# A decoder block's 512-column matmuls issued as two of 256

## The chip, the core and the metric

The kernel runs on one core of a Trainium2 chip. A time is the device time of one execution in microseconds. A core has five engines with a queue of instructions each: TensorE (PE, and PEld for its weight loads), VectorE (DVE), ScalarE (ACT), GpSimd (POOL) and SyncE (SP), which issues nearly all transfers.

## The reference

One decoder block on 512 tokens of 1024 channels, in float32. Two attention branches work on the same normalised and modulated input; their projections are gated and merged, then follow an output projection, an MLP with squared ReLU and a final norm.

```python
ada = (silu(c) @ w_ada + b_ada)          # sh1, sc1, g1, sh2, sc2, g2
h = modulate(rms_norm(x, ln1_w), sh1, sc1)
mq, mk, mv, rq, rk, rv, rg, ga, gr = split(h @ w_in)
y_a = moba_attention(rope(mq), rope(mk), mv) @ w_moba_o      # 8 heads of 64
r_out = head_group_norm(retention(rope(rq), rope(rk), rv), ret_gn_w)
y_r = (silu(rg) * r_out) @ w_ret_o                           # 8 heads, V of 128
x = x + g1 * ((sigmoid(ga) * y_a + sigmoid(gr) * y_r) @ w_out)
h2 = modulate(rms_norm(x, ln2_w), sh2, sc2)
x = x + g2 * (square(relu(h2 @ w_ff1)) @ w_ff2)
return rms_norm(x, final_norm_w)
```

## The kernel before

**Products.** Every large product is made from a hi and a lo part of both operands, float32 numbers rounded for TensorE and what that leaves out. mm3 (line 211) issues the three terms hi x hi, hi x lo and lo x hi, one matmul each, into the same accumulator, a tile of 128 partitions x 512 float32, which is one bank of PSUM. The stationary operand is always 128 x 128, the moving one mostly 512 columns. The matmul's flag `start` opens an accumulation and `stop` closes it. No product names its weight load: each matmul brings its own.

**Weights.** load_w (line 175) brings 128 x 1024 numbers by SP's queue into `raw`, ScalarE makes the hi part (line 179) and GpSimd the lo part (line 181), in four buffers each.

**Stages.** In the start (to about 78 us) adaLN's shift and scale are summed on VectorE, h is made tile by tile, and the first projections (V of MoBA, one pair of Q and K) run as h comes in (lines 334 to 370). Then comes the MoBA attention (lines 868 to 889, to about 275 us): for each of 8 heads and 4 key tiles, moba_turn transposes probabilities and splits them into th and tl, moba_scores makes the next head's softmax, and moba_values multiplies th and tl with V. Between them `fill(n)` issues n steps of the projections that wait in a queue, 6 products of 512 columns a step (line 422), and `do_later(n)` issues n pieces of the rotary embedding and of the stacking of Q and K (lines 459 to 510). The retention (lines 903 to 937, to about 475 us) goes the same way. Its V (ret_values, line 600) is made by products of 256 columns, two token tiles side by side in a bank. After it come the merge with the first half of the output projection (lines 950 to 975), the second half with the second norm (1075 to 1095), the MLP's first product, channel by channel (1097 to 1132; its first four tiles are issued in two halves of 256 tokens, lines 1097 to 1102, by ff1_part), and its second, token by token (1149 to 1202), into eight banks at once: 28 k-tiles for all tokens, then the last 4 for one token tile after the other with the final norm. The last token tile's second half is taken in two parts of 256 columns (line 1201).

**What sets the order.** The order of each engine's instructions is fixed when the program is built. Within `manual_schedule` the named engines keep the order of the program's text: TensorE from the start to the end of the retention and again from the output projection's second half to ff1's halves; VectorE, ScalarE and GpSimd in the start, VectorE and ScalarE in the second of these too. Elsewhere a planner picks, from the instructions that its own model has ready, the one that stands first in the program's text. `tc.high_priority(offset=20)` (line 574) moves what moba_turn's split issues forward by 20 places in that count, over all engines. `tc.issue_after` queues work behind a given instruction.

Of the kernel before, what the change touches and what calls it, by code (L numbers as in the profile page):

```python
# [22 lines left out]
# columns of w_in  # L23
# [4 lines left out]
def block_kernel(  # L28
# [101 lines left out]
    def busy(n):  # L130
        """Keeps the tensor engine's clock up while the first operands come in."""
        for _ in range(n):
            PE.matmul(warm, ones, wide, start=True, stop=True)
# [56 lines left out]
    def load_256(w, k0, c0):  # L190
        """Rows of 4 k-tiles, 256 columns."""
        hi, lo = load_w([(lambda t: v3(t, 256), rows(w, k0, 4, c0, 256))])
        return v3(hi, 256), v3(lo, 256)

    def load_pair(w, k0, ca, cb, lo_engine=None):
        """Rows of 4 k-tiles, two groups of 128 columns."""
        hi, lo = load_w(
            [
                (lambda t: v3(t, 256)[:, :, 0:P], rows(w, k0, 4, ca, P)),
                (lambda t: v3(t, 256)[:, :, P:256], rows(w, k0, 4, cb, P)),  # L200
            ],
            lo_engine=lo_engine,
        )
        return v3(hi, 256), v3(lo, 256)

    def load_512(w, k0, c0):
        """Rows of 2 k-tiles, 512 columns."""
        hi, lo = load_w([(lambda t: v3(t, 512), rows(w, k0, 2, c0, 512))])
        return v3(hi, 512), v3(lo, 512)

    def mm3(o, lh, ll, rh, rl, first, last):
        PE.matmul(o, lh, rh, start=first, stop=False)  # L212
        PE.matmul(o, lh, rl, start=False, stop=False)  # L213
        PE.matmul(o, ll, rh, start=False, stop=last)  # L214
# [8 lines left out]
    def token_rstd(work, ss, t, tag):  # L223
        """(mean of squares + eps) ** -0.5 from the sum of squares."""
        r = work.tile([P, 2], F32, name="rstd", tag=tag, bufs=4)
        POOL.tensor_scalar(r[:, 0:1], ss, 1.0 / D, EPS, op0=ALU.mult, op1=ALU.add)
        POOL.tensor_tensor(r[:, 1:2], r[:, 0:1], mhalf, op=ALU.pow)
        return r[:, 1:2]

# [1 line left out]
    def ada_cols(hi, lo, n0, dst):  # L231
        """Column sums of hi + lo over the partitions, as columns: 128 of them into dst[:, 0:2]."""
        PE.matmul(dst, hi[:, n0 : n0 + P], ones[:, 0:2], start=True, stop=False)
        PE.matmul(dst, lo[:, n0 : n0 + P], ones[:, 0:2], start=False, stop=True)
# [20 lines left out]
    def ada_start(j):  # L255
        """adaLN's shift and scale, summed over the k-tiles partition by partition, in two halves."""
        a = [ST.tile([P, 256], F32, name="adaacc", tag="adaacc", bufs=4) for _ in range(2)]
        for k in range(2):
            ACT.activation(a[k], ada[j][:, k, :], AF.Copy, scale=cact[:, k : k + 1])
        return a  # L260
# [9 lines left out]
    def ada_columns(a):  # L270
        """The sums over the partitions, as columns."""
        cp = ps("O")
        for i in range(2):
            PE.matmul(cp[:, 2 * i : 2 * i + 2], a[0][:, i * P : (i + 1) * P], ones32[:, 0:2], start=True, stop=True)
        return cp
# [58 lines left out]
    for j in range(NK):  # L334
        _, hi, lo = wf[j]
        more = j + 1 < NK
        if j + 2 < NK:
            load_step(j + 2)

        def product(i, a, b, first, last):  # L340
            """hi or lo of h by hi or lo of the weights, for V's four tiles of tokens, Q and K."""
            w = (hi, lo)[b]
            hx = (hh, hl)[a][j]
            if i < 4:
                PE.matmul(acc_mv[i], hx[:, i * P : (i + 1) * P], w[:, 0:512], start=first, stop=last)
            else:
                c0 = 512 if i == 4 else 640
                PE.matmul((acc_q0, acc_k0)[i - 4], w[:, c0 : c0 + P], hx, start=first, stop=last)

        if more:  # L350
            ada_sum(j + 1, a, range(2, 8))
            tp = transposed(j + 1)
        for i in range(6):
            product(i, 0, 0, j == 0, False)
        for i in range(6):
            product(i, 0, 1, False, False)
            if not more:
                product(i, 1, 0, False, True)
            elif i == 2:
                cp = ada_columns(a)  # L360
                mod = modulation(j + 1, cp)
        if more:
            w_split(j + 1)
            if j + 2 < NK:
                a = ada_start(j + 2)
            else:
                first_pair = [load_pair(w_in, k0, MQ + P, MK + P, eng) for k0, eng in ((0, POOL), (4, DVE))]
            h_tile(j + 1, tp, mod)
            for i in range(6):
                product(i, 1, 0, False, False)  # L370
# [17 lines left out]
    def proj_chunks(accs, ws, nk, bh, bl):  # L388
        """Two n-tiles, channel-major, from pieces of 4 k-tiles x 256 columns: 12 products a step."""
# [16 lines left out]
    # Projections are emitted in chunks between the steps of the attention, so that the tensor  # L406
    # engine has products to go on with while a step's scores pass through the other engines. A
    # projection is a generator: first its loads, then a chunk at a time.
# [8 lines left out]
    def fill(n):  # L417
        """n steps of the projections in the queue, 6 products of 512 columns each."""
# [7 lines left out]
    def project(load, nk, bh, bl, end):  # L426
        """Two n-tiles, channel-major, from pieces of 4 k-tiles x 256 columns, one after the other."""
# [24 lines left out]
    # Work that is not urgent, emitted a little at a time after a step's own instructions.  # L452
# [6 lines left out]
    def rope(i, part, a, stack):  # L459
        """Rotary embedding of a PSUM tile, then the stacking of its result."""  # L460
# [73 lines left out]
    def moba_scores(h, t):  # L534
        """Softmax of 128 queries of a head."""
# [13 lines left out]
        if t >= 2:  # L549
            # The past block counts where its gate, q . mean(k), is finite.  # L550
# [18 lines left out]
    def moba_turn(h, kt):  # L569
        """The probabilities of 128 keys, keys on the partitions, split."""  # L570
# [27 lines left out]
    vs = {}  # L598

    def ret_values(p):  # L600
        """V of 2 heads, token-major, less its mean over each head's channels: that centres the
        retention's output, which is linear in V, for the group norm."""
# [26 lines left out]
    # A window that picks output partitions n and n + 16, the sum of such two rows to copy to all, and  # L629
    # -1 where a row is to hold a lo part.  # L630
# [70 lines left out]
    def ret_variance(h, sh, sl):  # L701
        """The sum of squares over a head's channels, into rows 32 * (h % 4) and 16 further on."""
# [12 lines left out]
    def ret_rstd(g):  # L715
        """(variance + eps) ** -0.5 of 4 heads, hi in a head's first row and lo in its second."""
# [9 lines left out]
    def ret_norm(h):  # L726
        """A head's rows, added up, to all partitions; z, split."""
# [8 lines left out]
    # adaLN rows and columns that come later: g1, sh2, sc2 (and g2), 256 columns at a time. Each  # L736
    # step of the generator adds two k-tiles of one piece, loaded two steps before; a piece's sums
    # over the partitions follow a step after its last k-tile.
# [59 lines left out]
    def advance(steps, after=None):  # L798
        """One step, its arithmetic queued behind the instruction `after`."""
        try:  # L800
            steps.send(after)
        except StopIteration:
            pass
# [7 lines left out]
    def moba_out(i2):  # L811
        """sigmoid(ga) * (the MoBA branch's projection), two n-tiles: two projections."""
# [189 lines left out]
    def load_late(k):  # L1002
        """A k-tile of the second half of w_out, in the place of h."""
# [30 lines left out]
    def turn2(t):  # L1034
        """A normalized token tile to channels on the partitions, shifted and scaled."""
# [27 lines left out]
    # A token tile's transposition follows a good part of the products of the next ones.  # L1063
# [96 lines left out]
    def final(t, parts):  # L1160
        """The last terms of a token tile, residual and final norm, a part of the columns at a time."""
# [54 lines left out]
def _constants():  # L1216
    """Tables that depend on the shapes alone: rotary cos and signed sin (channel-major, two heads
    of 64), the retention's decay with its scale, the causal cap of a diagonal block, the identity."""
# [44 lines left out]
```

## Time and profile before

| | us |
|---|---|
| runs | 946.2, 950.24, 953.29 |
| median | 950.24 |
| span of the profiled execution | 943.5 |
| TensorE matmul, busy | 892.6 |
| TensorE weight load, busy | 716.0 |
| VectorE, busy | 549.0 |
| GpSimd, busy | 425.8 |
| ScalarE, busy | 365.7 |

The span goes from the first to the last instruction of one execution; the profile lists no other time of that execution. Matmuls are pipelined: a matmul's row gives its start and a modelled end that reaches over the next one's start, so the pace of a sequence is read from its starts, and a busy share of 100% says only that no gap was longer than that overlap. The weight load of the next matmul lies beside the one that runs. PEclk is the clock granted to TensorE, as a share of 2.4 GHz; its other level, 0.5, is 1.2 GHz.

### The profile page before, as it was taken

What the parts mean: (1) busy time and instruction counts of PE and PEld (TensorE: products, weight loads), DVE (VectorE), ACT (ScalarE), POOL (GpSimd) and SP (SyncE); (2) the same over time, 40 slices, a digit from 0 to 9 for tenths busy, and PEclk for the clock granted to TensorE, in tenths of its full rate; (3) what the DMA queues carried; (4) which work ended last, traced back from release to release, by engine and by line L of the source; (5) the groups of instructions that cost most, each with busy time, mean ns of one, the idle gap of its engine ahead of it and who ended that gap; (6) DMA issues with size and microseconds to landing.
All of it is one profiled execution on the core that took longest, in us unless ns stands there. A gap on an engine that the chain in (4) does not pass through costs nothing.

```text
span 943.5 us, 11349 instructions
## 1 busy us (share of the span) xinstructions
PE 892.6 (95%) x4138; PEld 716.0 (76%) x4138; DVE 549.0 (58%) x964; ACT 365.7 (39%) x617; POOL 425.8 (45%) x231
## 2 busy tenths in 40 slices
PE   6888999988999999989999898999999999999996
PEld 4766777667877878767888687888888888888885
DVE  5877887889796787996448867701423012211135
ACT  5444555554543434544531433422222321211124
POOL 4453242233353333433453633866566554444443
PEclk9998999899999999999999998999999999999999
DMA  9944121121135424341254362533432223222212
GB/s 288 296 147 124 46 90 45 67 89 46 45 118 164 135 87 145 109 130 52 90 176 151 126 240 81 170 107 93 148 117 89 90 90 106 95 89 90 93 42 89
DMA packets 104423, 108.38 MB, mean 115 GB/s; under 512 B 4832, under 2 KB 93232, under 8 KB 104368
## 3 DMA queue, kind: packets, MB, share of 16 engines
q1 hardware_dynamic: 104224, 107.41, 35.9%
q8 instruction: 32, 0.52, 0.2%
q10 hardware_dynamic: 144, 0.26, 0.1%
q14 instruction: 23, 0.19, 0.1%
HBM read 105.55 MB, written 2.10 MB: 114 GB/s over the span
## 4 chain that ended last, share of the span: by engine, by line
PE 61%; DVE 24%; DMA 5%; issue 4%; ACT 3%; POOL 1%; SPq 1%; ACTq 0%; POOLq 0%; DVEq 0%
PE ps_acc L212 16%; PE ps_acc L213 15%; PE ps_acc L214 15%; DVE adaacc L264 2%; DMA ada_raw<-in_w_ada_dram 2%; DVE qs L489 2%; PE ps_S L214 2%; PE ps_S L213 2%; PE ps_S L212 2%; DVE qs L490 2%; DVE kl L506 1%; DVE tl L221 1%; DVE pr L560 1%; DMA raw<-in_w_ff_dram 1%; ACT sw L466 1%
## 5 line engine op out<-in xcount | busy, mean ns | idle before, releaser
L181 POOL TENSOR_TENSOR wlo<-raw,whi 128x1024 fp32r<-128x1024 f32 x125 | 307.3, 2463 | 338.5 <-ACT whi L179 310.5
L179 ACT ACTIVATE whi<-raw 128x1024 fp32r<-128x1024 f32 x126 | 132.5, 1057 | 206.9 <-PE ps_O L214 108.7
L212 PE MATMUL ps_acc<-hh,whi 128*128 128x512 f32 x304 | 127.4, 419 | 0.4 <-DVE mod L763 0.4
L214 PE MATMUL ps_acc<-hh,wlo 128*128 128x512 f32 x304 | 121.3, 399 | 0.0
L213 PE MATMUL ps_acc<-hl,whi 128*128 128x512 f32 x304 | 120.8, 397 | 0.0
L212 PE MATMUL ps_acc<-h2h,whi 128*128 128x512 f32 (+1 forms) x288 | 107.3, 373 | 0.0
L213 PE MATMUL ps_acc<-h2l,whi 128*128 128x512 f32 (+1 forms) x288 | 107.2, 372 | 0.0
L214 PE MATMUL ps_acc<-h2h,wlo 128*128 128x512 f32 (+1 forms) x288 | 107.0, 371 | 0.0
L220 DVE CAST fh<-act 128x512 fp32r<-128x512 f32 x32 | 14.9, 472 | 138.4 <-PE ps_O L213 138.4
L212 PEld LDWEIGHTS ps_acc<-hh,whi 128*128 128x128 f32 x304 | 58.2, 191 | 17.6 <-issue 5.1
L214 PEld LDWEIGHTS ps_acc<-hh,wlo 128*128 128x128 f32 x304 | 58.2, 192 | 13.6
L213 PEld LDWEIGHTS ps_acc<-hl,whi 128*128 128x128 f32 x304 | 58.4, 192 | 10.3
L213 PEld LDWEIGHTS ps_acc<-h2l,whi 128*128 128x128 f32 x288 | 54.9, 191 | 10.1 <-DVE h2l L221 0.2
L214 PEld LDWEIGHTS ps_acc<-h2h,wlo 128*128 128x128 f32 x288 | 54.9, 191 | 10.1
L212 PEld LDWEIGHTS ps_acc<-h2h,whi 128*128 128x128 f32 x288 | 55.0, 191 | 9.9
L755 DVE TENSOR_TENSOR g<-g,ps_acc 128x256 f32<-128x256 f32 x8 | 3.3, 417 | 88.9 <-PE ps_acc L754 88.9
L213 PE MATMUL ps_acc<-wlo,fh 128*128 128x512 f32 (+1 forms) x136 | 52.7, 387 | 0.0
L212 PE MATMUL ps_acc<-whi,fh 128*128 128x512 f32 (+1 forms) x136 | 52.7, 387 | 0.0
L214 PE MATMUL ps_acc<-whi,fl 128*128 128x512 f32 (+1 forms) x136 | 52.6, 387 | 0.0
L779 DVE SCALAR_TENSOR_TENSOR ada_acc<-ada_raw,cact,ada_acc 128x256 f32<-128x256 f32 x48 | 36.5, 760 | 21.4 <-DMA ada_raw<-in_w_ada_dram 20.4
L1115 POOL TENSOR_TENSOR act<-relu 128x512 f32<-128x512 f32 x32 | 34.9, 1094 | 29.9 <-ACT relu L1114 29.9
L782 DVE SCALAR_TENSOR_TENSOR ada_acc<-ada_raw,cact,ada_acc 128x256 f32<-128x256 f32 x64 | 44.7, 699 | 1.7
(283 smaller groups left out, 1924.5 us busy)
## 6 DMA issues: line engine op xcount, KB each, us to landing
raw<-in_w_ff_dram SPq DMA_DIRECT2D x64, 512.0 KB, 3.3
raw<-in_w_in_dram SPq DMA_DIRECT2D x32, 512.0 KB, 3.5
ada_raw<-in_w_ada_dram SPq DMA_DIRECT2D x64, 256.0 KB, 2.7
raw<-in_w_in_dram SPq DMA_DIRECT2D x36, 256.0 KB, 3.4
wada<-in_w_ada_dram SPq DMA_DIRECT2D x32, 256.0 KB, 5.2
x<-in_x_dram SPq DMA_DIRECT2D x8, 512.0 KB, 4.6
raw<-in_w_ret_o_dram SPq DMA_DIRECT2D x8, 512.0 KB, 3.4
dec<-in_k_decay_dram SPq DMA_DIRECT2D x8, 256.0 KB, 3.7
```

What stands on the lines that cost most here:

```text
L179: ACT.activation(hi, raw, AF.Copy)
L181: eng.tensor_sub(lo, raw, hi.bitcast(F32))
L212: PE.matmul(o, lh, rh, start=first, stop=False)
L213: PE.matmul(o, lh, rl, start=False, stop=False)
L214: PE.matmul(o, ll, rh, start=False, stop=last)
L220: eh.tensor_copy(hi, src)
L264: DVE.scalar_tensor_tensor(a[k % 2], ada[j][:, k, :], cact[:, k : k + 1], a[k % 2], op0=ALU.mult, op1=ALU.add)
L489: DVE.tensor_copy(q[own, s, :], t[own, :])
L490: DVE.tensor_sub(q[other, s, :], t[own, :], q[own, s, :].bitcast(F32))
L779: eng.scalar_tensor_tensor(acc, raw[:, 0, :], cact[:, 2 * k2 : 2 * k2 + 1], acc, op0=ALU.mult, op1=ALU.add)
L782: eng.scalar_tensor_tensor(acc, raw[:, 1, :], cact[:, 2 * k2 + 1 : 2 * k2 + 2], acc, op0=ALU.mult, op1=ALU.add)
L1115: POOL.tensor_mul(act[n], r, r)
```

## The change

mm3 and the first projections go through a new helper, product_256, which issues a product in parts of at most 256 columns, one after the other, with the same stationary operand. Only the first part of the first term carries `start`, and only the last part of the last term `stop`. Products of 256 columns or fewer come out as they were. The attention's scores, values and transposes, adaLN's sums and the start's filler matmuls (`busy`) don't go through the helper. The diff's other lines take out comments and docstrings and are left out here.

```diff
+    def product_256(o, l, r, first, last):
+
+
+        n = r.shape[-1]
+        for c0 in range(0, n, 256):
+            c1 = min(c0 + 256, n)
+            PE.matmul(o[:, c0:c1], l, r[:, c0:c1], start=first and c0 == 0, stop=last and c1 == n)
+
     def mm3(o, lh, ll, rh, rl, first, last):
-        PE.matmul(o, lh, rh, start=first, stop=False)
-        PE.matmul(o, lh, rl, start=False, stop=False)
-        PE.matmul(o, ll, rh, start=False, stop=last)
+        product_256(o, lh, rh, first, False)
+        product_256(o, lh, rl, False, False)
+        product_256(o, ll, rh, False, last)
...
             if i < 4:
-                PE.matmul(acc_mv[i], hx[:, i * P : (i + 1) * P], w[:, 0:512], start=first, stop=last)
+                product_256(acc_mv[i], hx[:, i * P : (i + 1) * P], w[:, 0:512], first, last)
             else:
                 c0 = 512 if i == 4 else 640
-                PE.matmul((acc_q0, acc_k0)[i - 4], w[:, c0 : c0 + P], hx, start=first, stop=last)
+                product_256((acc_q0, acc_k0)[i - 4], w[:, c0 : c0 + P], hx, first, last)
```

## Rows read from the trace of the kernel before

**Rows 1.** the page's head and its first part, busy time by engine

```profile
span 943.5 us, 11349 instructions
PE 892.6 (95%) x4138; PEld 716.0 (76%) x4138; DVE 549.0 (58%) x964; ACT 365.7 (39%) x617; POOL 425.8 (45%) x231
```

**Rows 2.** stretches: busy us (x instructions) of PE PEld DVE ACT POOL, PEclk, DMA share, GB/s

```profile
78.00:275.00 197.00, 178.57 (x842) 140.09 (x840) 168.41 (x384) 101.34 (x217) 66.77 (x33) 0.95 0.22 69
...
475.00:530.00 55.00, 55.00 (x240) 44.22 (x239) 37.64 (x52) 14.68 (x21) 25.51 (x13) 1.00 0.50 167
530.00:575.00 45.00, 38.33 (x174) 30.52 (x173) 34.51 (x48) 16.60 (x30) 20.96 (x12) 0.96 0.50 171
575.00:600.00 25.00, 25.00 (x204) 24.82 (x205) 19.84 (x31) 9.57 (x19) 11.39 (x8) 0.94 0.35 107
600.00:755.00 155.00, 155.00 (x670) 125.13 (x669) 38.91 (x41) 45.75 (x59) 99.58 (x57) 1.00 0.37 115
755.00:900.00 145.00, 145.00 (x623) 116.22 (x622) 28.05 (x50) 28.88 (x28) 63.83 (x28) 1.00 0.27 95
900.00:944.00 44.00, 36.00 (x167) 29.36 (x165) 18.00 (x32) 14.15 (x32) 19.37 (x13) 0.96 0.17 60
```

**Rows 3.** the chain of waits by line, of 78-275, 275-330, 330-475, 475-530, 575-944 us

```profile
by line: PE ps_acc L212 8.9%; PE ps_acc L213 7.4%; PE ps_acc L214 7.1%; DVE qs L490 6.5%; DVE pr L560 6.1%; DVE kl L506 5.9%; DVE qs L489 5.7%; DVE tl L221 4.4%; ACT sw L466 3.7%; issue 3.3%; DVE stat L556 3.3%; DVE roped L478 3.0%; PE ps_S
...
by line: PE ps_acc L212 25.0%; issue 22.0%; PE ps_acc L214 21.9%; PE ps_acc L213 21.8%; POOL wlo L181 6.2%; PE ps_S L680 4.9%; PE ps_O L689 2.3%; PE ps_O L690 2.3%; PE ps_S L679 2.3%; PE ps_O L688 2.1%; PE ps_acc L234 0.8%; PE ps_PT L709 0.
...
by line: PE ps_acc L212 16.9%; PE ps_acc L214 15.0%; PE ps_acc L213 14.9%; issue 11.0%; DVE qs L489 3.0%; PE ps_S L680 2.6%; DVE tl L221 2.4%; DVE ada_acc L782 2.3%; DVE kh L502 2.0%; DVE sl L221 2.0%; DMA ada_raw<-in_w_ada_dram 1.8%; DVE a
...
by line: DMA ada_raw<-in_w_ada_dram 31.6%; DVE ada_acc L779 10.0%; DVE ada_acc L782 10.0%; DMA raw<-in_w_out_dram 10.0%; DVE ml L959 6.5%; issue 5.5%; DVE m L957 5.2%; POOL wlo L181 4.7%; POOL wol L221 4.7%; PE ps_acc L212 2.5%; PE ps_acc L
...
by line: PE ps_acc L213 24.4%; PE ps_acc L214 24.4%; PE ps_acc L212 24.3%; PE ps_S L214 4.1%; PE ps_S L213 4.0%; PE ps_S L212 4.0%; PE ps_PT L214 2.0%; PE ps_PT L213 2.0%; PE ps_PT L212 2.0%; PE ps_O L214 1.8%; PE ps_O L212 1.8%; PE ps_O L2
```

**Rows 4.** PE in time: start us, us; first and last of 43 starts, ff1 and ff2

```profile
645.02 0.40 PE L214 MATMUL ps_acc<-h2h,wlo 128*128 128x512 f32 x1
...
654.82 0.39 PE L214 MATMUL ps_acc<-h2h,wlo 128*128 128x512 f32 x1
...
800.15 0.39 PE L212 MATMUL ps_acc<-whi,fh 128*128 128x512 f32 x1
...
809.96 0.39 PE L212 MATMUL ps_acc<-whi,fh 128*128 128x512 f32 x1
```

**Rows 5.** PE in time, ff1's halved tiles: first and last of 82 starts

```profile
589.77 0.28 PE L214 MATMUL ps_acc<-h2h,wlo 128*128 128x256 f32 x1
...
598.95 0.28 PE L214 MATMUL ps_acc<-h2h,wlo 128*128 128x256 f32 x1
```

**Rows 6.** PE in time, retention's V (33 starts), last token tile (23 starts)

```profile
366.76 0.28 PE L212 MATMUL ps_acc<-whi,hh 128*128 128x256 f32 x1
...
370.53 0.28 PE L214 MATMUL ps_acc<-whi,hl 128*128 128x256 f32 x1
...
933.13 0.28 PE L213 MATMUL ps_acc<-wlo,fh 128*128 128x256 f32 x1
...
935.72 0.28 PE L214 MATMUL ps_acc<-whi,fl 128*128 128x256 f32 x1
```

**Rows 7.** PE in time, output projection: first and last of 10 starts

```profile
546.71 0.39 PE L213 MATMUL ps_acc<-wol,mh 128*128 128x512 f32 x1
...
548.75 0.39 PE L213 MATMUL ps_acc<-wol,mh 128*128 128x512 f32 x1
```

**Rows 8.** DMA queues: packets, MB, share of 16 engines; TensorE's instruction queue

```profile
q8 instruction: 32, 0.52, 0.2%
```

**Rows 9.** 78-275 us: VectorE's groups (busy us, mean ns), and one of PE's waits

```profile
L221 DVE TENSOR_TENSOR tl<-ps_PT,th 128x512 fp32r<-128x512 f32 (+3 forms) x32 | 15.4, 481 | 0.5 <-ACT th L218 0.3
...
L490 DVE TENSOR_TENSOR qs<-roped,qs 64x512 fp32r<-64x512 f32 x12 | 14.2, 1180 | 0.4
...
PE ps_O L582 <- DVE tl L221: 4.7, 6, 1.3
```

## The prediction

> **What bounds the kernel now.** I read the page's head first: TensorE is busy 95% of a span of 943.5 us, VectorE 58%, and 4138 matmuls stand beside as many weight loads, so every matmul carries a load of its own [rows 1]. The share is an average over unlike stages, so next I read the stretches and the chain of waits of each. In the MoBA stage (78 to 275 us) TensorE is busy 178.6 of 197 us, but VectorE 168.4, and only 23.4% of the chain lies in the products of lines 212 to 214; the rest is VectorE and ScalarE work between them [rows 2, 3]. From 275 to 475 us the products hold 68.7% of 55 us and 46.8% of 145 us. In the merge (475 to 530) the chain runs over adaLN's loads (31.6%) and VectorE, though TensorE never rests, and from 530 to 575 TensorE is busy 38.3 of 45 us. From 575 to the end TensorE is busy without a break but for the last 8 us, and lines 212 to 214 with their accumulators make up nearly the whole chain [rows 2, 3]. There a nanosecond per product is a nanosecond of the kernel; elsewhere it is mostly one of waiting.
>
> **The change, part by part.** mm3 and the first projections now issue each product of 512 columns as two of 256. Products that are 256 wide already stay: the retention's V (384), the first four tiles of ff1 (192) and the last 512 columns of the last token tile (24). Split are 144 of the first projections, 912 + 96 channel-major ones, 192 of the merge, 96 + 96 of the output projection, 672 of ff1 (28 tiles x 8 x 3) and 672 + 84 of ff2: 2964. In the stage that TensorE bounds it is 672 + 756 = 1428.
>
> What a product costs is read from starts, since the ends are modelled. In ff2 42 steps take 9.81 us, in ff1 42 take 9.80: 233.3 ns each, with the clock at 1.00, its 2.4 GHz level [rows 2, 4]. Products of 256 columns run in the same program: in ff1's halved tiles 81 steps take 9.18 us, 113.3 ns each [rows 5]. Two are 226.7 ns, 6.7 less than one of 512. But 256 has a second pace: 32 steps of the retention's V take 3.77 us, 117.8 ns, without a wait among them, and 22 at the very end take 2.59 us, 117.7 ns [rows 6]. Two of those are 235.6 ns, 2.3 more than one of 512. And 512 has a faster pace as well: in the output projection 9 steps take 2.04 us, 226.7 ns [rows 7], just twice 113.3. So it isn't the width alone; a stretch settles in a pace and keeps it.
>
> For ff1 I take 113.3, since its halves have the same operands and the same accumulators and follow directly upon rows 5: 672 x 6.7 = 4.5 us saved (bounds: +1.5 lost, 4.5 saved). For ff2 the nearest rows are those of the last tile, with the same operands at 117.7, but they lie among the final norm's work; the others speak for 113.3. I take two parts of 113.3 and one of 117.8, 114.8 a half, 229.6 a product: 756 x 3.7 = 2.8 us saved (bounds: 1.7 lost, 5.1 saved). From 275 to 475 us the chain has 37.8 + 67.9 = 106 us of products, some 460; paces of both widths mix there, so the gain lies between 2.3 lost and 6.7 saved each, 1.1 us lost to 3.1 saved; I take 0.5. Before 275 us and in 475 to 575 I take 0: what TensorE saves it waits longer for VectorE or a load (cover gone, the 232 products of the merge would give 1.5 us).
>
> The added loads cost nothing in the sum: at 113.3 ns per matmul as many loads as matmuls went by (205 beside 204 in the stretch from 575 to 600 us) without slowing it [rows 2]. Both halves read the same weights; a mm3 of 256 already loads the same ones twice running. The 5928 added instructions have to be fetched: today's 0.52 MB on TensorE's instruction queue take 0.2% of the DMA engines [rows 8], which would become some 0.9 MB and under 0.4%, beside a DMA share of 0.27 to 0.37 in the last stages; the 256-wide stretch shows no break for it, and without that cover a fetch of about 1 us (an estimate from 0.2% of 16 engines' span over 32 packets) for each of 23 more would be 23 us. No wait is added: a consumer still waits for the last matmul of its group, and its modelled end, 0.113 + 0.28 us after the pair's start, is that of the single one, 0.39 [rows 4, 5].
>
> Sum: 4.5 + 2.8 + 0.5 = 7.8 us off the profiled execution, a span of 935.7. The profile gives no other time of that execution; the median of the runs is 950.24, 6.7 us above the span, which the change does not touch. That is **942.4 us**, 0.8% less.
>
> Of fixed costs, rows 4 and 5 say that a narrow matmul has none over a wide one: 233.3 less 113.3 is 120 ns for 256 more columns, and 256 columns alone took less than that. The Trainium skill ("TensorE: Matmul & The Clock Gate", section "Back-to-back issue gap") speaks against the change: it gives a warm isolated gap of N / 2.4 + 2.5 ns, so two halves would pay the 2.5 twice. The rows disagree with its size, 215.8 ns for 512 columns against 233.3 measured. By it the last stage would lose 1428 x 2.5 = 3.6 us, an estimate from that page, and the time would be 953.8.
>
> **Rivals.** *Everything at the fast pace.* All halves settle at 113.3, as 81 steps did amid busy VectorE, ScalarE and GpSimd: 1428 x 6.7 = 9.5 us, with 460 x 6.7 = 3.1 of the middle at most and some of the merge, about 12 in all: 938 us. Against it stand rows 6.
>
> *The slow pace, or a price per instruction.* The fast rows owe their pace to something else than their width, as rows 7 hint, and the pairs settle at 117.8, or pay anew for each instruction: 1428 x 2.3 = 3.3 us lost, 953.5 us. For it stands the last tile, which has ff2's operands. It decides above 116.7 a half. The page's rule just named belongs here, and its size falls into the same case.
>
> *The planner's order, slower.* The order on VectorE and ScalarE comes from the planner, and moba_turn gives its split a rewind of 20 instructions (line 574). Today the 20 reach back over about 3 transposes, a piece of rotary work, 2 value products, 6 products and another such piece. With 12 products in place of 6 they end before the second piece, so that this can go ahead of the split on VectorE, and TensorE's value products wait behind the split: today VectorE's tl costs them 4.7 us in 6 waits [rows 9]. A piece like qs costs 1.18 us [rows 9]; for 20 of the 32 turns that is 23.6 us, less the 7.8 gained: 966 us. It becomes slower by 1% from 15 turns on (17.3 us). Against it: such a piece is ready long before, and mostly done while 12 products run.
>
> **How the numbers follow.** The forecast has 0.44, everything fast 0.26, the slow pace 0.18, the planner's order 0.12. A measurement of this kernel tells about 1% (9.5 us) from no change. Faster by that is below 940.7: all of the second case but 0.02, and the lower end of the first (0.08), 0.32. Slower is above 959.7: 0.11, and 0.01 for unforeseen fetch stalls, 0.12. Within 1%: 0.56. For the range I reach down to 937, where everything is fast, and up to 955, past the slow pace; the planner's case is left out, with the corners. The forecast's own range is 939 to 947, by ff2's two bounds and the middle's.
>
> **What would show it.** Right: in ff1 and ff2 two starts lie 0.23 us or less apart per pair, most often 0.227, the stretch from 575 us to the end is 7 to 8 us shorter, about 7100 matmuls and as many loads stand on the page, and TensorE's waits in the MoBA stage grow a little with its length unchanged. The weight loads are then near 100% busy from 575 us, harmlessly. The forecast is wrong if a pair takes 0.2356 us through ff2, if breaks of about 1 us come every 256 instructions, if the MoBA stage (78 to 275 us) is longer by several us with waits for tl, or if the front stages gain more than 3 us.

## The result and the profile after

The changed kernel takes **956.0 us** (median of 10 runs, 951.4 to 959.8) against 949.3 us of the kernel before in the same batch: ratio 1.0071, interval 1.0045 to 1.0096. A second batch gave 1.0097 (1.006 to 1.0134). So it is 7 to 9 us slower where 8 us less was forecast. The page's head and the line of TensorE's instruction queue answer to [rows 1, 8]:

```profile
span 954.1 us, 17277 instructions
PE 898.4 (94%) x7102; PEld 861.5 (90%) x7102; DVE 555.4 (58%) x964; ACT 366.2 (38%) x617; POOL 425.7 (45%) x231
...
q8 instruction: 55, 0.90, 0.4%
```

The change did what it says: 2964 more matmuls, each with its load. The fetch grew as worked out, from 32 to 55 packets. The stretches, in the columns of [rows 2]:

```profile
78.00:275.00 197.00, 178.76 (x1267) 161.97 (x1265) 165.06 (x381) 101.57 (x216) 67.15 (x33) 0.95 0.23 69
475.00:530.00 55.00, 55.00 (x472) 54.86 (x471) 32.76 (x47) 13.98 (x20) 24.48 (x12) 1.00 0.45 144
530.00:575.00 45.00, 40.21 (x323) 40.00 (x322) 31.40 (x42) 17.42 (x29) 21.89 (x13) 0.92 0.55 183
575.00:600.00 25.00, 21.91 (x166) 21.55 (x165) 20.50 (x36) 8.12 (x19) 9.37 (x6) 0.86 0.26 76
600.00:755.00 155.00, 155.00 (x1354) 155.00 (x1353) 54.02 (x48) 47.99 (x63) 101.71 (x58) 1.00 0.40 119
755.00:900.00 145.00, 145.00 (x1237) 145.00 (x1236) 25.75 (x46) 28.96 (x29) 65.86 (x30) 1.00 0.32 95
```

From 600 to 900 us the loads are busy all the time and TensorE has no gap. A busy share of 100% says nothing of the pace, so the starts decide. The view of TensorE in time (start, duration, line, operation) puts neighbouring matmuls of one kind in a row: "x2" is a pair, what was one product of [rows 4]. First and last of 45 rows and of 43 in ff1, of 44 in ff2 and of 38 in the output projection:

```profile
644.87 0.39 PE L217 MATMUL ps_acc<-h2l,whi 128*128 128x256 f32 x2
...
654.84 0.39 PE L217 MATMUL ps_acc<-h2h,whi 128*128 128x256 f32 x2
...
669.76 0.40 PE L217 MATMUL ps_acc<-h2l,whi 128*128 128x256 f32 x2
...
679.65 0.40 PE L217 MATMUL ps_acc<-h2l,whi 128*128 128x256 f32 x2
...
799.81 0.40 PE L217 MATMUL ps_acc<-wlo,fh 128*128 128x256 f32 x2
...
809.94 0.40 PE L217 MATMUL ps_acc<-whi,fl 128*128 128x256 f32 x2
...
556.95 0.40 PE L217 MATMUL ps_acc<-wol,mh 128*128 128x256 f32 x2
...
565.83 0.40 PE L217 MATMUL ps_acc<-woh,ml 128*128 128x256 f32 x2
```

That is 9.97 / 44 = 226.6 ns, 9.89 / 42 = 235.5, 10.13 / 43 = 235.6 and 8.88 / 37 = 240.0 ns for what took 233.3 [rows 4] and, in the output projection, 226.7 [rows 7]. Both paces of 256 columns that [rows 5, 6] showed are there, and each lasts for tens of microseconds. In ff1 the fast one (113.3 ns a half) holds to 665.0 us, the slow one (117.8) to 687.9, the fast one to 709.9, the slow one to 732.8 and the fast one to the end of ff1, 765.7: each change stands at a pair of adaLN's sums (lines 761 and 762). At the border to ff2 it turns slow and stays so to the last four k-tiles, which take 116.7 ns a half. The loads are as many at either pace, and at the fast one two halves with two loads take less time than one wide product.

Which pace ff1 begins in differs between executions. Its halved tiles [rows 5], the same products in all 17 traces of this study, run at 113.3 ns in eight and at 117.8 in nine. In a trace whose program is that of the kernel before up to ff2 (the probes in the kernel before, below), 81 steps take 9.54 us:

```profile
594.44 0.28 PE L214 MATMUL ps_acc<-h2h,wlo 128*128 128x256 f32 x1
...
603.98 0.28 PE L214 MATMUL ps_acc<-h2h,wlo 128*128 128x256 f32 x1
```

Where ff1 is split too and carries no extra products, it goes on in the pace of these tiles to the first pair of sums. The changed kernel's own two traces are among those that began fast.

**Where the time went**, by the starts of named products. The traces of this study give each stage several times, with its products whole or split, so I compare means; the two runs that reorder the first head (below), and ff1 and ff2 where products of zeros stand in them or ff2's order or place was changed, are left out:

| stretch | whole, us | split, us | difference |
|---|---|---|---|
| from the first product of the queue (at about 70 us) to the first transpose of pr | 36.6 (7) | 38.9 (8) | +2.2 |
| MoBA, to the retention's first value product | 161.9 (7) | 163.6 (8) | +1.7 |
| retention, to its last value product | 180.3 (7) | 182.7 (8) | +2.4 |
| from there to the merge | 25.5 (7) | 25.9 (8) | +0.5 |
| merge | 56.2 (7) | 56.3 (8) | +0.1 |
| output projection, to ff1 | 46.2 (6) | 47.8 (9) | +1.6 |
| ff1 | 182.6 (5) | 180.9 (9) | -1.7 |
| ff2 | 178.96 (5) | 180.62 (3) | +1.7 |

(In brackets the number of traces; of the output projection both forms occur with either attention.) The sum is 8.5 us, between the two ratios' 6.7 and 9.2. Of it 6.8 lie ahead of the merge, where I had costed nothing or a small gain. The four first rows together are 401.8 to 406.8 us whole and 408.0 to 412.8 split: they don't overlap.

Two rows are means over unlike executions. Split ff1 takes 178.4 to 179.9 us in the four traces that begin fast and 181.6 to 183.2 in the five that begin slow, where nothing is saved. The whole retention takes 178.0 to 178.2 us in three traces and 181.7 to 182.1 in four, with the same instructions in the same order on VectorE, ScalarE and GpSimd; the longer ones hold a longer wait of TensorE for the group norm. That wait in the kernel before, in the run with ff1 alone split, and in the changed kernel:

```profile
PE ps_PT L708 <- DVE zf L731: 0.6, 1, 0.6
PE ps_PT L719 <- DVE zf L742: 3.6, 1, 3.6
PE ps_PT L716 <- DVE zf L739: 2.0, 1, 2.0
```

The retention's 2.4 us is thus less certain than the sum of the four rows.

In the attention two things are seen. The products are slower: a projection's 18 products in a row, 17 steps, of the kernel before and then of the changed one:

```profile
293.65 0.40 PE L212 MATMUL ps_acc<-hh,whi 128*128 128x512 f32 x1
...
297.55 0.39 PE L214 MATMUL ps_acc<-hh,wlo 128*128 128x512 f32 x1
```

```profile
295.94 0.40 PE L217 MATMUL ps_acc<-hh,whi 128*128 128x256 f32 x2
...
299.94 0.40 PE L217 MATMUL ps_acc<-hh,wlo 128*128 128x256 f32 x2
```

3.90 us against 4.00, 229.4 ns a product against 235.3. Over all products at full clock with no wait behind them it is 229 to 232 ns whole and 234 to 236 split; for the 1008 products of the four first rows that is 114 x 5.7, 336 x 4.4, 456 x 3.5 and 102 x 4.5 ns, 4.2 us in all, some of it beside waits. And the clock is at its low level more often: of the stretch from 80 to 475 us 30.3 us in the mean of the split traces against 22.4 in the whole ones, by the trace's record of the clock. At half the speed 7.9 us more of that lose at most 4.0. Two stretches of the kernel before, then of the changed one (PEclk is the third number from the end):

```profile
104.00:118.00 14.00, 13.09 (x58) 9.51 (x57) 11.55 (x28) 5.99 (x15) 1.72 (x1) 1.00 0.25 75
...
405.00:440.00 35.00, 32.79 (x135) 24.36 (x134) 30.73 (x46) 16.76 (x29) 16.22 (x9) 0.95 0.31 98
```

```profile
104.00:118.00 14.00, 11.44 (x74) 9.86 (x73) 10.88 (x27) 4.40 (x12) 2.35 (x1) 0.88 0.24 73
...
405.00:440.00 35.00, 30.89 (x203) 27.72 (x203) 28.47 (x46) 15.46 (x26) 13.70 (x7) 0.90 0.30 96
```

Both drops follow on waits: TensorE is busy 11.4 of the first 14 us where it was 13.1. Of the waits from 78 to 275 us, two lines of the changed kernel, the first answering to the last of [rows 9], and then the second's counterpart in the kernel before:

```profile
PE ps_O L590 <- DVE tl L229: 3.8, 5, 1.3
PE ps_PT L581 <- DVE pr L568: 2.6, 1, 2.6
```

```profile
PE ps_PT L573 <- DVE pr L560: 0.6, 1, 0.6
```

The wait for tl is no longer than before; the one for pr is, 2.6 us against 0.6. The planner did reorder VectorE's instructions: from the first head's softmax on, about 155 of 964 stand at another place. There a rotary group of five pieces now stands ahead of the last pr.

Before the output projection's second half one wait of 4.8 us takes the place of two of 1.1 and 1.7, and the low clock goes with it (a pair takes 0.43 us; the high level is back at 552.7 us). Over all traces the clock falls there in nine of nine with the attention split and in four of eight with it whole:

```profile
542.61 0.39 PE L217 MATMUL ps_O<-whi,ml 128*128 128x256 f32 x2
547.79 0.80 PE L217 MATMUL ps_S<-whi,mh 128*128 128x256 f32 x2 [4.79 <-ACT mh L966]
548.38 0.63 PE L217 MATMUL ps_S<-wlo,mh 128*128 128x256 f32 x2
548.81 0.63 PE L217 MATMUL ps_S<-whi,ml 128*128 128x256 f32 x2
```

### The profile page after: what moved, and what is told of

The parts are those of the page before. It is cut to its first block, busy times and chain, and to the rows that moved or that the text cites. A ratio compares the mean times of both kernels' runs of the same rounds, so it can differ in the third digit from the quotient of the medians.

```text
span 954.1 us, 17277 instructions
## 1 busy us (share of the span) xinstructions
PE 898.4 (94%) x7102; PEld 861.5 (90%) x7102; DVE 555.4 (58%) x964; ACT 366.2 (38%) x617; POOL 425.7 (45%) x231
## 4 chain that ended last, share of the span: by engine, by line
PE 62%; DVE 22%; DMA 6%; ACT 4%; issue 3%; SPq 1%; POOL 1%; ACTq 0%; DVEq 0%; POOLq 0%
PE ps_acc L217 47%; PE ps_S L217 6%; DMA ada_raw<-in_w_ada_dram 3%; PE ps_PT L217 3%; PE ps_O L217 2%; DVE qs L498 2%; DVE ada_acc L790 2%; DVE adaacc L272 1%; DVE qs L497 1%; DMA wada<-in_w_ada_dram 1%; DVE kl L514 1%; DVE ada_acc L787 1%; DMA raw<-in_w_in_dram 1%; DVE tl L229 1%; ACT sw L474 1%
## 5 line engine op out<-in xcount | busy, mean ns | idle before, releaser
L217 PE MATMUL ps_acc<-hh,whi 128*128 128x256 f32 x608 | 128.9, 294 | 1.7 <-DVE mod L771 1.0
L217 PE MATMUL ps_acc<-hl,whi 128*128 128x256 f32 x608 | 122.7, 283 | 0.0
L217 PE MATMUL ps_acc<-hh,wlo 128*128 128x256 f32 x608 | 122.2, 282 | 0.0
L217 PE MATMUL ps_acc<-h2h,whi 128*128 128x256 f32 x512 | 106.7, 280 | 0.0
L217 PE MATMUL ps_acc<-h2l,whi 128*128 128x256 f32 x512 | 106.6, 279 | 0.0
L217 PE MATMUL ps_acc<-h2h,wlo 128*128 128x256 f32 x512 | 106.3, 279 | 0.0
L217 PEld LDWEIGHTS ps_acc<-hh,whi 128*128 128x128 f32 x608 | 95.7, 192 | 9.7 <-issue 5.1
L228 DVE CAST fh<-act 128x512 fp32r<-128x512 f32 x32 | 15.1, 478 | 136.7 <-PE ps_O L217 136.7
L217 PE MATMUL ps_acc<-whi,fl 128*128 128x256 f32 x264 | 53.3, 281 | 0.0
L217 PE MATMUL ps_acc<-wlo,fh 128*128 128x256 f32 x264 | 53.2, 281 | 0.0
L217 PE MATMUL ps_acc<-whi,fh 128*128 128x256 f32 x264 | 53.2, 281 | 0.0
```

The lines of the kernel that those rows point to most:

```text
L217: PE.matmul(o[:, c0:c1], l, r[:, c0:c1], start=first and c0 == 0, stop=last and c1 == n)
L228: eh.tensor_copy(hi, src)
```

## The experiments

Ratios are to the kernel before in the same batch. Where an experiment adds products, they are by a tile of zeros into an accumulation that is open, so the output stays what it was.

**The second product whole again.** In the changed kernel `ff2_step` and `final` call a form of mm3 with single matmuls.

```diff
-            mm3(yo[half][t], fh[:, ts], fl[:, ts], whi[:, hs], wlo[:, hs], k == 0, last and half == 1)
+            mm3w(yo[half][t], fh[:, ts], fl[:, ts], whi[:, hs], wlo[:, hs], k == 0, last and half == 1)
```

> The changed kernel with ff2's 756 products wide again. Theory (a stretch of matmuls settles in one of two paces, 113.3 or 117.8 ns per half, and what comes just before decides which; in ff2 it is the slow one): ff2, from its first to its last start, falls from 180.6 to 179.0 us and the kernel gains 1.7 us, 954.3. Rival (every product split costs 2.3 ns more, wherever it is: 2964 of them make the 6.7 us lost): the same 1.7 us here, 954.3. Rival (the planner's order in the attention costs the 6.7 us, the products nothing): no change, 956. This run sizes ff2's part.

Measured: 1.0116 (1.0076 to 1.0155). ff2 comes back from 180.62 to 178.96 us in the trace, but the kernel is no faster than the changed one. Of the three expectations only "no change" is near, but 1.7 us lie within the spread from run to run; most of the loss must be elsewhere.

**ff1 alone split**, in the kernel before.

```diff
-            mm3(a[:, cs], hi, lo, h2h[:, k, cs], h2l[:, k, cs], k == 0, k == NK - 1)
+            mm3n(a[:, cs], hi, lo, h2h[:, k, cs], h2l[:, k, cs], k == 0, k == NK - 1)
```

> The kernel before with ff1's 672 products alone split. Theory of two paces: ff1 (first to last h2 product) falls from 182.2 us to between 178 and 181, since it begins in the fast pace behind its own halved tiles, and the kernel gains 1.5 to 4.5 us, 945 to 948 against 949.3. Rival of a price per split product: 672 x 2.3 ns = 1.5 us lost, 950.8. Rival of the planner's order: nothing, 949.3.

Measured: 1.0015 (0.9989 to 1.0041), ff1 183.2 us in its trace. No gain, and the ratio is the one of the price per split product (950.7 us beside 949.3, where the rival had 950.8). But here ff1 was at the slow pace from 587 to 660 us, turned fast at the first pair of adaLN's sums, back at the second, and so on to the fourth. The very same products went the other way round in the changed kernel, at 113.3 ns, which a price for each product doesn't allow.

**Probes.** If a pace is held until something breaks the sequence, a few odd matmuls must be able to turn it. The changed kernel with zero products of several widths ahead of six k-tiles of ff2:

```diff
+    probes = {4: (256,), 8: (256, 256), 12: (256, 256, 256), 16: (128,), 20: (128, 128), 24: (512,)}
...
+        if k in probes:
+            for n in probes[k]:
+                PE.matmul(yo[0][0][:, 0:n], nil, w[0][:, 0:n], start=False, stop=False)
```

> The changed kernel with some extra matmuls by zeros added into ff2's first accumulator: one of 256 columns before k-tile 4, two before 8, three before 12, one of 128 before 16, two of 128 before 20, one of 512 before 24. Theory of two paces chosen by what comes before: at some of these the pace of a half flips between 117.8 and 113.3 ns and then stays for the 192 matmuls to the next; each stretch of four k-tiles at the fast pace saves 0.86 us, up to 5 us in all. Rival of operands or of a price per instruction: the pace stays at 117.8 throughout, and the kernel is about 1 us slower for the ten extra matmuls.

Measured: 1.0138 (1.0104 to 1.0172), ff2 181.1 us. One, two or three of 256 and one of 128 turn nothing; two of 128 turn ff2 from 117.8 to 113.3 ns a half for the next 192 matmuls, and one of 512 turns it back.

The same probes in the kernel before:

> The kernel before, ff2 wide, with the same extra matmuls by zeros at the same k-tiles as the earlier probe. Theory of two paces: wide products obey the same, so after the two of 128 columns before k-tile 20 the step falls from 233.3 to about 226.7 ns and stays to k-tile 24, 0.6 us less in that stretch. Rival (only narrow products have two paces, a wide one of ff2 always takes 233.3): every stretch keeps 233.3.

Measured: 951.55 us in one run. Products of 512 columns keep 233.3 ns behind every probe: none of these probes turns them in ff2.

The changed kernel with pairs of 128 ahead of k-tiles 3, 7 and 11, then three and four of them, and two of 512:

> The changed kernel with other extra matmuls by zeros in ff2: two of 128 columns before k-tiles 3, 7 and 11, three of 128 before 15, four of 128 before 19, two of 512 before 23. Theory of two paces chosen by what comes before: the first pair takes the halves from 117.8 to 113.3 ns as in the earlier probe; if a pair swaps the two, the second takes them back and the third over again; if it always leads to the fast one, all three stretches run at 113.3. Rival (the flip there was chance): the three stretches differ without a pattern, or stay at 117.8.

Measured: 949.19 us in one run. The first pair turns ff2 to the fast pace, and none of the later ones turns it back; ff2 takes 177.2 us. The operands, the accumulators and the main instructions are those of the changed kernel, so the slow pace belongs to none of these alone.

**ff2's operands elsewhere**: the changed kernel with 64 bytes ahead of fh and fl.

```diff
+    F2.tile([P, 16], F32, name="pad")
     yo = [[ps("acc") for _ in range(NT)], [ps("S"), ps("S"), ps("PT"), ps("O")]]
```

> The changed kernel with 64 bytes of padding ahead of ff2's activations in SBUF, which shifts the stationary operands by 64 bytes against the weights and changes no instruction. Rival that the place of the operands in memory sets the pace: ff2's halves leave 117.8 ns for another steady value. Theory that what comes before sets it: they stay at 117.8 or go to 113.3, and nothing else.

Measured: 960.6 us in one run; ff2 182.2 us, in a third steady pattern of about 118.7 ns a half. So the place of the operands counts too; fh and fl are the stationary ones. The output projection's steady 120.0 ns may be of this kind; that wasn't tried.

**The order of the halves**: three terms of the first half of the bank, then three of the second.

```diff
+        for c in (slice(0, 256), slice(256, 512)):
+            PE.matmul(o[:, c], lh, rh[:, c], start=first and c.start == 0, stop=False)
+            PE.matmul(o[:, c], lh, rl[:, c], start=False, stop=False)
+            PE.matmul(o[:, c], ll, rh[:, c], start=False, stop=last and c.start == 256)
```

> The changed kernel with ff2's six matmuls in another order: three terms of the first half of the bank, then three of the second, as many matmuls and loads. If it is the alternation of the two halves that makes the slow pace, ff2 leaves 117.8 ns a half and takes 174 to 176 us. If the pace is only what the sequence fell into before, it comes out at one of the two known paces, 174 or 180.6 us, as at the entry, and stays there. If each matmul has a price, it stays at 180.6 us.

Measured: ff2 180.62 us, 117.8 ns a half. The alternation of the halves is not what makes the slow pace; that the pace is set at the border fits, and by this run alone so would a price per matmul. It isn't inherited from ff1: here and in the changed kernel ff1 ended fast, in the first probe slow, and ff2 begins slow in every trace in which both are split. In the one with ff2 alone split (below) it begins fast.

**The changed kernel once more**, in the second batch:

> The changed kernel once more, beside the others on one chip. Whatever the theory, ff2 takes 180.6 us from first to last start; ff1 (179.9 us in its profile, but 181.9 to 183.2 in the three others that split it) tells whether its pace differs from execution to execution: the theory of two paces set by what comes before lets it, a price per instruction doesn't. The kernel is 0.7% slower than the one before, as measured.

Measured: 1.0097 (1.006 to 1.0134); its trace shows the same pattern of paces in ff1 and ff2. ff1 takes 178.5 us. So its pace does differ from execution to execution: in the traces of 182 to 183 us the same products began slow.

**The attention whole**, all else as in the changed kernel: the first projections and the queue of projections by single matmuls of 512.

> The changed kernel with the first projections and all that the attention's queue issues wide again (1152 products); merge, output projection, ff1 and ff2 stay split. Theory of two paces: the attention's products ran at 233.5 ns a pair against 230.6 wide, 1110 x 2.9 = 3.2 us, of which some is on the chain; with the planner's order restored too, 2 to 5 us gained, 951 to 954. Rival of the planner's order alone: all of the 6.7 us comes back, 949.3. Rival of a price per split product: 1152 x 2.3 = 2.6 us, 953.4.

Measured: 1.0043 (1.0023 to 1.0064), which puts 953.4 us beside 949.3. The first run that takes part of the loss away, but not all of it, so the planner's order alone is out. The time is that of a price per split product (953.4), and within the range of the other theory. ff1 began slow in this trace (182.8 us), so what is left split has a loss of its own here.

**The attention and the merge alone split**, all behind them whole:

```diff
-                mm3(wo0[t], mh[k][:, ts], ml[k][:, ts], hi[:, k % 2, :], lo[:, k % 2, :], k == 0, k == NK - 1)
+                mm3w(wo0[t], mh[k][:, ts], ml[k][:, ts], hi[:, k % 2, :], lo[:, k % 2, :], k == 0, k == NK - 1)
...
-            mm3(a, mh[k][:, ts], ml[k][:, ts], hi, lo, k == 0, k == NK - 1)
+            mm3w(a, mh[k][:, ts], ml[k][:, ts], hi, lo, k == 0, k == NK - 1)
```

(and the same in ff1 and ff2)

> The changed kernel with all behind the merge as single matmuls of 512 columns: the output projection, ff1 and ff2. What stays split are the first projections, the attention's and the merge's. If the attention carries most of the loss, as the stages of the traces add up (about 2 us each ahead of the MoBA stage, in it and in the retention, at 234 to 235 ns per 512 columns against 230, and more time at the lower clock), the kernel is 5 to 7 us slower than the one before, ratio 1.005 to 1.0075. If TensorE's pace there only shortens its waits, as the prediction costed it, the ratio lies within 0.002 of 1.

Measured: 1.0094 (1.0061 to 1.0127), 6 to 12 us. The front by itself costs as much as the whole change. That what stands behind it balances holds only where ff1 begins fast: in the run before this one it lost 2 to 6 us. The two ratios add up to more than the change cost, within their intervals.

**The output projection alone split**, in the kernel before, at the two places of the last diff:

> The kernel before with the output projection's products alone split (both halves of it, 192 products). By the account of the traces this part loses 1.2 us in the second half, at a steady 120.0 ns a half, and up to 2 us between the last merge product and it: ratio 1.001 to 1.004. If that loss came with the attention's change and not with these products, the stretch ahead of the second half stays at 15.6 to 17.5 us and the ratio is 1.001.

Measured: 1.0004 (0.9981 to 1.0028). 24.65 us against 23.4 for its second half, as expected, but the stretch ahead of it stays at 15.1 us. The split of these products doesn't bring the long wait by itself. That the attention's change does isn't shown by one trace: the stretch takes 14.7 to 18.0 us in the eight traces with the attention whole, 16.6 and 17.4 with the attention split and these products whole, and 17.8 to 19.3 with both split.

**The planner's order.** In the kernel with the attention alone split, the rotary pieces are queued behind the first head's last softmax; `moba_scores` returns that instruction.

```diff
-        moba_scores(0, t)
+        done = moba_scores(0, t)
         fill(2)
-        do_later(2)
+        if t > 1:
+            do_later(2)
+        if t == 0:
+            with tc.issue_after(done):
+                do_later(4)
```

> The kernel with the attention's split alone, and in it the two groups of rotary pieces that the planner now puts ahead of the last two softmaxes of the first head are queued behind the last of them. If the planner's order costs the stretch ahead of the MoBA stage its 2 us (the wait for pr is 2.6 us in the changed kernel and 0.6 in the one before, with the lower clock behind it), that stretch comes down from 38.9 to 36 to 37 us, the wait to under 1 us, the drop of the clock near 110 us goes, and the ratio to the kernel before falls from 1.009 to about 1.006. If the pace of the products alone is to blame, the stretch stays above 38 us and the ratio where it was.

The control, the same in the kernel before:

> The control: the same reordering in the kernel before, whose order already has the softmaxes ahead of the rotary pieces there. By both theories it stays within 0.003 of the kernel before; if the reordering itself is worth something, the run with the split attention is to be held against this one.

Measured: 1.0093 (1.0061 to 1.0126), and 1.0033 (1.0014 to 1.0053) for the control. The stretch itself did as the order's theory says, from 38.9 to 36.1 us, the wait for pr is gone, and so is the drop of the clock behind it, as the same two stretches of the split form show:

```profile
104.00:118.00 14.00, 12.34 (x90) 10.74 (x88) 12.12 (x24) 7.32 (x14) 2.87 (x2) 1.00 0.25 75
405.00:440.00 35.00, 29.86 (x211) 26.40 (x211) 29.87 (x48) 16.54 (x29) 14.39 (x8) 1.00 0.31 98
```

The ratio to the kernel before did not fall. But the reordering by itself costs 0.3% in the control, and held against it, as the control's expectation asks, the ratio is 1.006 (about 1.002 to 1.010): what the order's theory named, and not to be told from 1.009. The runs spread from 950.8 to 959.0 us, and the trace is of one of 951.8. In it the clock is at its high level through the whole retention, which still takes 181.1 us against the control's 177.9 with a drop in it; since the whole form alone gives 178 or 182 us, that doesn't settle the clock's part. How the loss divides between pace, order and clock stays open.

**Making use of it.** The kernel before with ff2 alone split, and a pair of zero products of 128 columns ahead of the second k-tile:

```diff
+        if k == 1:
+            for _ in range(2):
+                PE.matmul(yo[0][0][:, 0:P], nil, w[0][:, 0:P], start=False, stop=False)
```

> The kernel before with ff2 alone split, and two products of 128 columns by a tile of zeros into an open accumulator ahead of the second k-tile. If ff2's pace is one of two that the sequence falls into and keeps, the two short products bring it to 113.3 ns a half until about the last four k-tiles: ff2 from its first to its last main product 173 to 176 us against 179.0 in the kernel before, the time 3 to 5 us less, ratio 0.995 to 0.997. If the slow pace belongs to ff2's operands or is a price of each instruction, ff2 stays at 117.8 ns, 180.6 us, and the ratio is 1.001 to 1.003.

Measured: 0.996 (0.9936 to 0.9985), 945.2 us against 948.8, as expected; ff2 174.8 us. In its trace ff2 was at the fast pace already at the border, so this run shows the gain and not the pair's part in it.

ff1 split too, with such a pair behind each of adaLN's sums:

```diff
-                PE.matmul(cp[:, 0:256], ones, lo, start=False, stop=True)
+                PE.matmul(cp[:, 0:256], ones, lo, start=False, stop=not nudge)
+                for i in range(2 if nudge else 0):
+                    PE.matmul(cp[:, 0:P], nudge[0], hi[:, 0:P], start=False, stop=i == 1)
```

> The kernel before with ff1 and ff2 split, two short products of zeros after each pair of adaLN's sums in ff1 and the two in ff2. If short products always lead to the fast pace, ff1 runs at 113.3 ns a half throughout, 177.5 us against 182.2 in the kernel before, and ff2 takes 173 to 176: 8 to 10 us less in all, ratio 0.990 to 0.992. If they only flip whatever pace there is, ff1 stays mixed (179 to 182 us) and the gain is that of ff2 alone at best.

Measured: **0.9944** (0.9911 to 0.9976), 941.5 us against 948.8: the lowest time of all, faster than both kernels, though less than expected, and its interval overlaps the last one's. ff1 began fast in this trace and stays at 113.3 ns behind all four pairs of sums, where it turned slow at two of them in the changed kernel; with the low clock at its start it takes 179.1 us. At the border ff2 begins slow, and the pair turns it; ff2 takes 175.0 us. TensorE in time at that turn:

```profile
760.72 0.40 PE L220 MATMUL ps_acc<-wlo,fh 128*128 128x256 f32 x2
...
761.66 0.40 PE L220 MATMUL ps_O<-whi,fl 128*128 128x256 f32 x2
761.90 0.34 PE L1174 MATMUL ps_acc<-whi,nil 128*128 128x128 f32 x2
762.07 0.45 PE L220 MATMUL ps_acc<-whi,fh 128*128 128x256 f32 x2
...
762.60 0.39 PE L220 MATMUL ps_acc<-whi,fl 128*128 128x256 f32 x2
...
763.96 0.39 PE L220 MATMUL ps_acc<-whi,fl 128*128 128x256 f32 x2
```

Four pairs take 0.94 us ahead of the short products, six take 1.36 behind them: 235 ns and 227 ns with the same operands.

## Why the prediction was wrong

Wrong in direction. "A stretch settles in a pace and keeps it" held until something else stood between the products, and the counts, the loads and the fetch came as worked out. What failed, step by step:

- *Before 275 us taken as 0, because TensorE's gain would be waited away.* This is the largest miss: 3.9 us lost there in the stage account, and with the retention and what follows to the merge 6.8. I asked only what a gain would be worth; the split products are slower there (235 ns against 230), waits and time at the low clock grew, and this wasn't waited away. The forecast of 0.5 us saved from 275 to 475 us became 2.9 lost, beyond its bound of 1.1: longer waits and the clock were not in the bound, nor that the retention differs by 4 us between executions. Which of the causes takes how much is not shown.
- *ff2 at two parts 113.3 and one part 117.8.* It ran at 117.8 up to the last four k-tiles, 1.7 us lost where 2.8 saved was forecast: exactly the bound that its nearest rows gave [rows 6], and the sign on record as the one that would refute the forecast. Mixing the two paces was no estimate: ff2 is in one or the other.
- *ff1 at 113.3 throughout*, 4.5 us saved, came to 1.7 in the mean: adaLN's sums, whose place the trace of before shows, turn the pace each time, and rows 5 were one of two cases. That the trace of before had the fast one is luck of that execution.
- *475 to 575 us at 0*: 1.7 us lost, by a longer wait with the low clock and by the output projection at 120.0 ns a half, which no row of before showed.
- *The 6.7 us around the span* were no such thing: nearly all runs stand 1.7 to 1.9 us above their own spans, 3.3 at most (945.46 and 943.7 in the run with ff2 alone split); the rest was the difference between executions.

Of the rivals, the *slow pace* came nearest, 953.5 against 956.0, with ff2's term right and ff1's wrong in sign. Its other reading, a price for each instruction, falls: the same matmuls take 113.3 ns behind a pair of short ones. Here belongs the rule of the Trainium skill ("TensorE: Matmul & The Clock Gate", section "Back-to-back issue gap"): by its formula for a warm isolated gap, 2.5 ns for each further matmul would be 953.8, an estimate from that page and close by. But the matmuls of this trace take 113.3, 117.8 or 120.0 ns where the rule has 109.2 for all, so its nearness is chance. *The planner's order* was right in that the order changed and cost about 2 us at one place; but not by the rewind of 20 (with 26 in its place the changed kernel's program comes out the same) and not by waits for tl, and 966 us was far off. *Everything fast* is nearly what the short products make of ff1 and ff2: worth 7.3 us by the medians, 2 to 8 by the ratio's interval, with the front left whole.

## What to carry to other kernels

Before a product is split or merged, read the starts of long stretches of either form, in the traces of several executions: one trace shows one case only. Where one form shows two paces, let the two be the range and one of them the value, never their mean. Cost a loss in stages where TensorE waits as well as a gain. An edit of a matmul's form that a planner sees also moves other engines' work; leave such stages as they are and change only the one that TensorE bounds, as the two runs that were faster did.

## What the runs showed of the hardware

At the 2.4 GHz level a sequence of 256-column matmuls runs at 113.3 or at 117.8 ns a matmul with the same operands, for up to 160 us on end. Which of the two a stretch begins in can differ between executions of the same products (ff1's halved tiles: 8 traces to 9). A few matmuls of another kind turn it: two of 128 columns by another stationary tile led from the slow pace to the fast one each time (ff2 in three kernels), a single one of 512 once back to the slow one; two of 512 did not. Shifting the stationary operand by 64 bytes gave a third pace of 118.7 ns in one run. Single matmuls of 512 columns stayed at 233.3 ns in ff2 behind every probe. What in the chip holds a pace isn't shown by these runs, nor whether the loads that each matmul brings have a part in it.
